# Six of the 31 taps of one depthwise convolution, moved from VectorE to float32 products with diagonal matrices on TensorE

## The chip, the core and the metric

The kernel runs on one core of a Trainium2 chip. The core has five engines that work side by side, each through its own queue in order: TensorE (PE; its weight loads are listed apart as PEld), VectorE (DVE), ScalarE (ACT), GpSimd (POOL) and SyncE (SP), which issues the DMAs. They share an on-chip memory (SBUF); TensorE writes its sums into a second one (PSUM), which VectorE and ScalarE read. The metric is device time in microseconds (us), the median of several runs.

## The reference

Two layers of a streaming encoder over 1024 prompt frames and 8 x 16 sample frames, model width 1024. Each layer computes, cut to what matters here:

```python
h = rms_norm(x, g1)
q, k, v, a, b = split(h @ w_in)
u = a * sigmoid(b)                              # 512 channels
A = sink_attention(q, k, v)                     # 8 heads, chunks of 64 frames, window 128
y = depthwise_conv31(u, conv_w) + conv_b        # causal, 31 taps, each channel by itself
C = silu(layer_norm(y))
x = x + concat(beta_a * A, beta_c * C) @ w_out
x = x + relu(rms_norm(x, g2) @ w_up) ** 2 @ w_down
```

The depthwise convolution is `y[c, t] = sum_k w[k, c] * u[c, t + k] + b[c]`, with 30 frames of state ahead of the first. For a fixed k it is the product of a 128x128 diagonal matrix, w[k] on the diagonal, with the 128 channels' frames shifted by k.

## The kernel before

Activations lie transposed, channels on the 128 partitions, frames along the free dimension. The 1152 frames are three blocks (b = 0, 1, 2) of 384. Everything is float32; for the large products each operand is split into a rounded part and a remainder (`h[0]`, `h[1]`; `u[:, 0]`, `u[:, 1]`), and `gemm` (L213 to L215) runs three one-pass products for each 128 rows of depth, 24 products of 128x384 for one output tile. A weight tile arrives by DMA (L204), ScalarE rounds it (L205), GpSimd takes the remainder (L206); six buffers hold the halves.

The first layer begins with `rmsnorm` of blocks 0 and 1 (L268 to L285). Then, by the program's text: `glu` of block 0 (eight gemms, the gate, the tile U of 4 channel tiles with 30 frames of halo ahead; L320 on GpSimd writes it), `make_qkv` of blocks 0 and 1, the attention of both, `glu` of blocks 1 and 2, `out(0)` (the product with w_out, then the norm `rmsnorm` of block 0 for the feed-forward), and the feed-forward of block 0 as filler.

The convolution is a generator that runs beside this in a "lane". `unit_done` is called after each gemm's unit of work and calls `tick`, which lets the generator at the head of each lane take `rate` steps: 6 for the first block of layer 0, 5 and 3 for the others (`CONV`). A step is one `yield`. In the kernel before, a step is one tap: a VectorE instruction that multiplies 384 shifted frames by the tap's weight (one scalar per partition) and adds them to the accumulator `acc` in PSUM. Tap 0 (L353) also adds the bias. After tap 30 ScalarE copies the accumulator over the first 384 columns of U (L358). The accumulator (tag "c") has one buffer, so the next channel tile waits for that copy. Four channel tiles of 31 taps make a block; then `conv_tail` does the layer norm and the SiLU, with the mean as a float32 product on TensorE (L659).

The text above isn't the order in which the engines work. The framework plans each engine's order ahead of the run from dependencies, the program's order as priority and its own estimates of durations (`schedule_with_timeline_sim=True`); the run then keeps that order on every engine. `after(t, self.pe)` orders a tap in this plan behind the latest gemm, without a wait in the run.

`hidden` (L704 to L707) is the first user of the tag "hid" (four buffers of 128x768), in the feed-forward.

Of the kernel before, what the change touches and what calls it, by code (L numbers as in the profile page):

```python
# [8 lines left out]
F32 = mybir.dt.float32  # L9
F32R = mybir.dt.float32r  # L10
AF = mybir.ActivationFunctionType
ALU = mybir.AluOpType
# [4 lines left out]
NCONV, CW, CS = 512, 31, 30  # L17
HD, NH, NKV = 64, 8, 2
EPS = 1e-6
NB, BT = 3, 384  # L20
# [15 lines left out]
MIX = ((0, 1, 1), (2, 0.9, 1.1))  # L36

CONV = ((6, 5, 3), (3.5, 3.5, 3.5))
TAIL = (3, 2)
ATT = ((0.5, 0.3, 0.3), (0.3, 0.35, 0.25))  # L40


G1, G2, QG, KG = 0, 8, 16, 17
CWT, CB, LNG, LNB = 18, 142, 146, 150
# [17 lines left out]
class Kernel:  # L62
# [235 lines left out]
    def glu(self, l, b, h, conv=None):  # L298
# [32 lines left out]
        if not last:  # L331
            self.halo = self.sp.tile([128, 4, CS], F32, tag="halo", name=self.nm("halo"), bufs=1)
            nc.gpsimd.tensor_copy(self.halo, U[:, :, BT:])

    def conv(self, l, b):

        nc = self.nc
        U = self.u[b]
        for ct in range(4):
            u = U[:, ct]  # L340
            if b < NB - 1:
                parts = [(lambda k: u[:, k:k + BT], slice(0, BT), lambda t: t)]
            else:
                us = u[:, UP:].rearrange("p (b s) -> p b s", s=SEG)
                parts = [(lambda k: u[:, k:k + 256], slice(0, 256), lambda t: t),
                         (lambda k: us[:, :, k:k + DEC_T], slice(256, BT), lambda t: t.rearrange("p (b s) -> p b s", s=DEC_T))]
            acc = self.pc()
            for k in range(CW):
                w = self.v(l, CWT + ct * CW + k)
                for src, s, view in parts:  # L350
                    o = view(acc[:, s])
                    if k == 0:
                        t = nc.vector.tensor_scalar(out=o, in0=src(k), scalar1=w, scalar2=self.v(l, CB + ct), op0=ALU.mult, op1=ALU.add)  # L353
                    else:
                        t = nc.vector.scalar_tensor_tensor(out=o, in0=src(k), scalar=w, in1=o, op0=ALU.mult, op1=ALU.add)  # L355
                    self.after(t, self.pe)
                if k == CW - 1:
                    nc.scalar.copy(u[:, :BT], acc)  # L358
                yield
        for _ in self.conv_tail(l, b):  # L360
            for _ in range(TAIL[l]):
                yield
# [659 lines left out]
    def run(self):  # L1022
        nc, tc, a = self.nc, self.tc, self.a
# [7 lines left out]
        x = [self.load_x(src[0])]  # L1031
        self.load_consts()
        x.append(self.load_x(src[1]))
        h1 = [self.rmsnorm(x[0], 0, G1), self.rmsnorm(x[1], 0, G1)]
        for l in range(DEPTH):
            self.u, self.co, self.k, self.vb = [None] * NB, [None] * NB, [], []
            x, h, ao = [None] * NB, [None] * NB, [None] * NB
            fin = l == DEPTH - 1
            nsrc = [a["y"][b] if fin else self.dp.tile([128, KT, BT], F32, tag=f"x{b}", name=f"xd{l}{b}") for b in range(NB)]
            kept = self.dp.tile([128, KT, BT], F32, tag=f"kept{l}", name=f"kept{l}")  # L1040
            nh = []
            alone, pair, place, mix, conv, att = (t[l] for t in (ALONE, PAIR, PLACE, MIX, CONV, ATT))

            def blk(b, end=False, x=x, h=h, nsrc=nsrc, nh=nh, l=l, fin=fin):
# [14 lines left out]
            with tc.tile_pool(name=f"ap{l}", bufs=1) as self.ap:  # L1059
                self.mix = 0  # L1060
                self.mix = mix[0]
                self.glu(l, 0, h1[0], conv)
                if l == 0:
                    for n in ("sk", "sv", "sc"):
# [3 lines left out]
                if l:  # L1068
                    self.glu(l, 1, h1[1], conv)
# [78 lines left out]
            h1, src = nh, nsrc  # L1148
# [120 lines left out]
```

## Time and profile before

| what | value |
|---|---|
| runs, median of 3 | 2387.7 us (2385.42 to 2388.78) |
| the profiled execution: its time, its span | 2387.42 us, 2385.6 us |
| PE busy | 2312.7 us, 97% of the span |
| DVE, POOL, ACT busy | 1676.6 us (70%), 1514.6 us (63%), 1269.3 us (53%) |
| mean granted TensorE clock | 0.995 of full speed |
| DMA | 266.49 MB, mean 112 GB/s |

The span is the time from the first to the last instruction in the trace; the execution's time is 1.8 us longer. A busy share is an average over the whole span; the work differs from stage to stage. Products overlap in TensorE, so that its busy time runs high: a gemm product lasts about 0.34 us by itself, while the next starts 0.17 us later. In a busy time by stretches, a column holds the busy us of one engine and, in brackets, its instructions. In a row of a timeline, the bracket at the end is the idle time of the engine just before and what ended it. "r", "g", "c" and "m" are tiles in PSUM, "f" and "t" scratch in SBUF.

### The profile page before, as it was taken

The page shows a single profiled execution, that of the slowest core. Times are in us where ns is not written, and L with a number is a line of the kernel's source. Part 1 is how long each engine was busy: PE and PEld are TensorE (multiplying, and loading weights), DVE is VectorE, ACT ScalarE, POOL GpSimd, SP SyncE. Part 2 cuts the span into 40 slices and gives each one's busy share as a digit, 9 for nine tenths or more (in the row PEclk, how much of TensorE's full clock was granted, in tenths as well). Part 3 has the DMA queues.
Part 4 walks back from the last instruction along what each step waited for, and adds up shares of the span by engine and source line. Part 5 has one row for each costly group of instructions (what it writes and reads, how often), then busy time and mean ns, then how long its engine had stood idle before and what let it go on. Part 6 is the DMA issues. An engine that isn't in the chain of part 4 may idle for free.

```text
span 2385.6 us, 39001 instructions
## 1 busy us (share of the span) xinstructions
PE 2312.7 (97%) x13822; PEld 2250.2 (94%) x13822; DVE 1676.6 (70%) x3153; ACT 1269.3 (53%) x2732; POOL 1514.6 (63%) x1247
## 2 busy tenths in 40 slices
PE   7999899999999999999999999999999999999999
PEld 7898898999989999999999999999999899999999
DVE  5999978996378777787687764799834877752222
ACT  5467546555335555644565566466433555544442
POOL 6975485656476665866856866856345666666662
PEclk9999999999999999999999999999999999999999
DMA  5423333434332223443334344434333122254442
GB/s 191 147 88 103 106 111 121 120 121 125 99 96 79 64 71 107 150 135 115 99 119 122 120 142 129 134 99 126 92 106 107 58 71 71 84 164 137 136 126 75
DMA packets 164260, 266.49 MB, mean 112 GB/s; under 512 B 24753, under 2 KB 55729, under 8 KB 164017
## 3 DMA queue, kind: packets, MB, share of 16 engines
q1 hardware_dynamic: 164064, 264.01, 35.8%
q8 instruction: 108, 1.77, 0.3%
q14 instruction: 88, 0.71, 0.1%
HBM read 250.19 MB, written 16.05 MB: 112 GB/s over the span
## 4 chain that ended last, share of the span: by engine, by line
PE 73%; DVE 18%; POOL 4%; issue 3%; DMA 2%; ACT 1%; DVEq 0%; POOLq 0%; SPq 0%; ACTq 0%
PE g L723 13%; PE g L213 12%; PE g L214 12%; PE g L215 12%; DVE c L355 6%; PE x L1006 4%; PE x L926 4%; PE g L1006 3%; PE m L723 2%; PE r L723 2%; PE g L926 2%; POOL w L893 2%; DMA A<-in_w 1%; PE c L723 1%; POOL w L206 1%
## 5 line engine op out<-in xcount | busy, mean ns | idle before, releaser
L206 POOL TENSOR_TENSOR w<-raw,w 128x512 fp32r<-128x512 f32 x728 | 972.7, 1347 | 599.5 <-ACT w L205 589.1
L205 ACT CAST w<-raw 128x512 fp32r<-128x512 f32 x728 | 445.1, 619 | 422.8 <-PE g L215 124.0
L213 PE MATMUL g<-h,w 128*128 128x384 f32 x1696 | 576.4, 341 | 8.2 <-ACT h L284 4.2
L214 PE MATMUL g<-h,w 128*128 128x384 f32 x1696 | 574.1, 339 | 0.6 <-DVE h L285 0.6
L215 PE MATMUL g<-h,w 128*128 128x384 f32 x1696 | 573.1, 338 | 0.0
L355 DVE SCALAR_TENSOR_TENSOR c<-u,vec,c 128x384 f32<-128x384 f32 (+1 forms) x960 | 498.0, 519 | 17.6
L723 PE MATMUL g<-hid,w 128*128 128x384 f32 x2304 | 429.1, 340 | 8.4 <-DVE x L725 5.3
L723 PEld LDWEIGHTS g<-hid,w 128*128 128x128 f32 x2304 | 397.8, 188 | 16.6 <-DVE x L725 9.5
L213 PEld LDWEIGHTS g<-h,w 128*128 128x128 f32 x1696 | 321.0, 189 | 12.4 <-ACT h L284 4.8
L214 PEld LDWEIGHTS g<-h,w 128*128 128x128 f32 x1696 | 321.0, 189 | 2.2 <-DVE h L285 1.0
L215 PEld LDWEIGHTS g<-h,w 128*128 128x128 f32 x1696 | 320.8, 189 | 0.9
L707 DVE TENSOR_TENSOR hid<-t,hid 128x384 fp32r<-128x384 f32 x128 | 107.5, 840 | 186.7 <-ACT hid L706 186.4
L893 POOL TENSOR_TENSOR w<-S,w 128x512 fp32r<-128x512 f32 x96 | 138.6, 1446 | 120.6 <-ACT w L892 120.3
L725 DVE TENSOR_TENSOR x<-x,g 128x384 f32<-128x384 f32 x240 | 130.0, 549 | 66.9 <-PE g L723 66.1
L704 ACT ACTIVATE t<-g 128x384 f32<-128x384 f32 x128 | 62.8, 491 | 148.2 <-PE g L215 147.7
L1006 PE MATMUL x<-F,w 128*128 128x384 f32 x624 | 120.4, 337 | 4.2 <-DVE x L1009 2.3
L893 POOL TENSOR_TENSOR w<-raw,w 128x512 fp32r<-128x512 f32 x64 | 90.5, 1414 | 41.9 <-ACT w L892 40.6
L1006 PEld LDWEIGHTS x<-F,w 128*128 128x128 f32 x624 | 109.3, 188 | 6.0 <-DVE x L947 2.5
L1006 PE MATMUL g<-F,w 128*128 128x384 f32 x528 | 107.6, 339 | 3.3 <-ACT F L815 1.4
L892 ACT CAST w<-S 128x512 fp32r<-128x512 f32 x96 | 59.7, 622 | 93.3 <-DVE S L879 48.2
L1006 PEld LDWEIGHTS g<-F,w 128*128 128x128 f32 x528 | 92.7, 188 | 7.1 <-ACT F L815 2.7
L893 POOL TENSOR_TENSOR w<-A,w 128x512 fp32r<-128x512 f32 x64 | 86.9, 1362 | 19.3 <-ACT w L892 19.1
(237 smaller groups left out, 4010.9 us busy)
## 6 DMA issues: line engine op xcount, KB each, us to landing
raw<-in_w SPq DMA_DIRECT2D x792, 256.0 KB, 2.7
A<-in_w SPq DMA_DIRECT2D x64, 256.0 KB, 2.7
x<-in_x SPq DMA_DIRECT2D x24, 384.0 KB, 5.0
x<-xd SPq DMA_DIRECT2D x12, 384.0 KB, 5.1
kept<-x SPq DMA_DIRECT2D x4, 768.0 KB, 4.0
x<-kept SPq DMA_DIRECT2D x8, 384.0 KB, 4.4
xd<-x SPq DMA_DIRECT2D x4, 768.0 KB, 4.9
out_y<-x SPq DMA_DIRECT2D x4, 768.0 KB, 4.4
```

The source lines that it names most:

```text
L205: nc.scalar.copy(u[:, 0], raw)
L206: nc.gpsimd.tensor_tensor(out=u[:, 1], in0=raw, in1=u[:, 0].bitcast(F32), op=ALU.subtract)
L213: nc.tensor.matmul(ps, lhsT=u(0, k), rhs=h(0, k), start=k == 0, stop=False)
L214: nc.tensor.matmul(ps, lhsT=u(0, k), rhs=h(1, k), start=False, stop=False)
L215: self.pe = nc.tensor.matmul(ps, lhsT=u(1, k), rhs=h(0, k), start=False, stop=k == KT - 1)
L355: t = nc.vector.scalar_tensor_tensor(out=o, in0=src(k), scalar=w, in1=o, op0=ALU.mult, op1=ALU.add)
L707: nc.vector.tensor_tensor(out=hid[:, 1], in0=f, in1=hid[:, 0].bitcast(F32), op=ALU.subtract)
L723: self.pe = nc.tensor.matmul(ps, lhsT=u(p), rhs=hid[:, q], start=i == 0, stop=i == n - 1)
L725: nc.vector.tensor_tensor(out=x[:, m], in0=x[:, m], in1=ps, op=ALU.add)
L893: nc.gpsimd.tensor_tensor(out=u[:, 1], in0=f[n], in1=u[:, 0].bitcast(F32), op=ALU.subtract)
L926: nc.tensor.matmul(ps, lhsT=u[:, p, k], rhs=H[h](q, k), start=start and k == 0 and i == 0, stop=k == 3 and i == 2, skip_group_check=True)
L1006: nc.tensor.matmul(o, lhsT=u[:, p, 2 * i + j], rhs=F(j, hn)[:, q], start=start and n == 0, stop=n == 5, skip_group_check=True)
```

## The change

Before the norm of block 1, `diagonal` builds four tiles of six 128x128 diagonal matrices, one for each channel tile: the identity times the weights of taps 0 to 5, both spread by broadcasting, in one VectorE instruction of 128x768. They lie in the four "hid" buffers. The convolution of layer 0, block 0, which is the first to find `self.diagonals` filled, takes for each channel tile one entry: six float32 products add taps 0 to 5 into the accumulator, VectorE adds taps 6 to 30 as before, and the copy becomes an activation that adds the bias. There is one more `yield` behind the products of each tile, and one ahead of the first tile. All other convolutions find the list empty and stay as they are.

```diff
--- before.py
+++ after.py
@@ -36,6 +36,7 @@
 MIX = ((0, 1, 1), (2, 0.9, 1.1))
 
 CONV = ((6, 5, 3), (3.5, 3.5, 3.5))
+TAPS = 6
 TAIL = (3, 2)
 ATT = ((0.5, 0.3, 0.3), (0.3, 0.35, 0.25))
 
@@ -332,6 +333,14 @@
             self.halo = self.sp.tile([128, 4, CS], F32, tag="halo", name=self.nm("halo"), bufs=1)
             nc.gpsimd.tensor_copy(self.halo, U[:, :, BT:])
 
+    def diagonal(self, ct):
+
+        n = TAPS * 128
+        d = self.hp.tile([128, 2, BT], F32R, tag="hid", name=self.nm("dg"), bufs=4).bitcast(F32).rearrange("p a b -> p (a b)")[:, :n].rearrange("p (k c) -> p k c", c=128)
+        w = self.v(0, CWT + ct * CW, TAPS)
+        self.nc.vector.tensor_tensor(out=d, in0=self.ident.unsqueeze(1).to_broadcast([128, TAPS, 128]), in1=w.unsqueeze(2).to_broadcast([128, TAPS, 128]), op=ALU.mult)
+        return d
+
     def conv(self, l, b):
 
         nc = self.nc
@@ -345,7 +354,15 @@
                 parts = [(lambda k: u[:, k:k + 256], slice(0, 256), lambda t: t),
                          (lambda k: us[:, :, k:k + DEC_T], slice(256, BT), lambda t: t.rearrange("p (b s) -> p b s", s=DEC_T))]
             acc = self.pc()
-            for k in range(CW):
+            taps = TAPS if self.diagonals else 0
+            if taps:
+                if ct == 0:
+                    yield
+                dg = self.diagonals.pop(0)
+                for k in range(taps):
+                    nc.tensor.matmul(acc, lhsT=dg[:, k], rhs=u[:, k:k + BT], start=k == 0, stop=k == taps - 1)
+                yield
+            for k in range(taps, CW):
                 w = self.v(l, CWT + ct * CW + k)
                 for src, s, view in parts:
                     o = view(acc[:, s])
@@ -355,7 +372,10 @@
                         t = nc.vector.scalar_tensor_tensor(out=o, in0=src(k), scalar=w, in1=o, op0=ALU.mult, op1=ALU.add)
                     self.after(t, self.pe)
                 if k == CW - 1:
-                    nc.scalar.copy(u[:, :BT], acc)
+                    if taps:
+                        nc.scalar.activation(u[:, :BT], acc, AF.Identity, bias=self.v(l, CB + ct))
+                    else:
+                        nc.scalar.copy(u[:, :BT], acc)
                 yield
         for _ in self.conv_tail(l, b):
             for _ in range(TAIL[l]):
@@ -1031,7 +1051,9 @@
         x = [self.load_x(src[0])]
         self.load_consts()
         x.append(self.load_x(src[1]))
-        h1 = [self.rmsnorm(x[0], 0, G1), self.rmsnorm(x[1], 0, G1)]
+        h1 = [self.rmsnorm(x[0], 0, G1)]
+        self.diagonals = [self.diagonal(ct) for ct in range(4)]
+        h1.append(self.rmsnorm(x[1], 0, G1))
         for l in range(DEPTH):
             self.u, self.co, self.k, self.vb = [None] * NB, [None] * NB, [], []
             x, h, ao = [None] * NB, [None] * NB, [None] * NB
```

## Rows read from the trace of the kernel before

**Rows 1.** The page: engine, busy us (share), instructions; the chain; a line's group.

```profile
PE 2312.7 (97%) x13822; PEld 2250.2 (94%) x13822; DVE 1676.6 (70%) x3153; ACT 1269.3 (53%) x2732; POOL 1514.6 (63%) x1247
...
PE 73%; DVE 18%; POOL 4%; issue 3%; DMA 2%; ACT 1%; DVEq 0%; POOLq 0%; SPq 0%; ACTq 0%
...
L206 POOL TENSOR_TENSOR w<-raw,w 128x512 fp32r<-128x512 f32 x728 | 972.7, 1347 | 599.5 <-ACT w L205 589.1
```

**Rows 2.** Busy us (instructions) of PE, PEld, DVE, ACT, POOL by stretch; granted clock, DMA.

```profile
25.00:75.00 50.00, 50.00 (x298) 49.69 (x297) 35.38 (x65) 28.74 (x51) 40.14 (x30) 1.00 0.58 187
75.00:186.00 111.00, 106.66 (x750) 98.59 (x748) 107.75 (x215) 67.71 (x177) 94.78 (x90) 0.97 0.32 97
186.00:290.00 104.00, 92.02 (x565) 87.22 (x565) 99.85 (x206) 67.79 (x167) 50.65 (x46) 0.94 0.37 111
300.00:540.00 240.00, 232.49 (x1450) 223.11 (x1450) 214.16 (x493) 140.02 (x351) 154.78 (x142) 1.00 0.39 118
```

**Rows 3.** The chain that ended last, by line, 25 to 75 us.

```profile
by line: PE g L214 32.5%; PE g L215 31.8%; PE g L213 31.6%; PE r L249 2.2%; PE r L255 1.2%; PE g L382 1.1%; PE g L445 0.4%
```

**Rows 4.** The chain that ended last, by line, 75 to 186 us.

```profile
by line: DVE c L355 43.3%; DVE t L295 6.4%; issue 6.3%; DVE t L293 6.1%; DVE h L285 4.8%; DVE t L292 4.0%; DVE f L283 4.0%; DVE s L500 3.9%; DVE s L503 3.0%; DVE s L506 2.6%; DVE pt L560 2.6%; DVE s L502 2.0%; DVE v L429 1.7%; DVE ao L574 1
```

**Rows 5.** The line of taps 1 to 30, 50 to 192 us: count, ns min/median/max.

```profile
L355 DVE SCALAR_TENSOR_TENSOR c<-u,vec,c x120: 594/622/624, 52.5 to 189.9; 128x384 f32<-128x384 f32 x120
```

**Rows 6.** The line of tap 0, 50 to 192 us.

```profile
L353 DVE TENSOR_SCALAR c<-u,vec x4: 668/670/680, 50.9 to 164.4; 128x384 f32<-128x384 f32 x4
```

**Rows 7.** ScalarE's copies of the accumulator, 50 to 200 us.

```profile
L358 ACT COPY u<-c x4: 468/476/491, 85.9 to 191.5; 128x384 f32<-128x384 f32 x4
```

**Rows 8.** VectorE in order of time: start us, us, instruction, idle before.

```profile
71.00 3.26 DVE L355 SCALAR_TENSOR_TENSOR c<-u,vec,c 128x384 f32<-128x384 f32 x5
75.36 0.62 DVE L283 SCALAR_TENSOR_TENSOR f<-x,vec,r 128x384 f32<-128x384 f32 x1 [1.10 <-PE r L255]
```

**Rows 9.** TensorE in order of time around the float32 product L659.

```profile
204.33 0.34 PE L214 MATMUL g<-h,w 128*128 128x384 f32 x1
204.51 0.81 PE L659 MATMUL r<-f,cst 128*128 128x384 f32 x2
204.86 0.63 PE L215 MATMUL g<-h,w 128*128 128x384 f32 x1
205.33 0.33 PE L213 MATMUL g<-h,w 128*128 128x384 f32 x1
```

**Rows 10.** Who TensorE waited for, 50 to 290 us: total us, times, longest.

```profile
PE m L568 <- DVE pt L560: 4.3, 4, 2.7
...
PE g L213 <- DVE s L446: 2.7, 1, 2.7
...
PE m L558 <- DVE og L572: 2.0, 5, 0.5
```

**Rows 11.** VectorE in order of time at the start.

```profile
8.82 0.17 DVE L179 TENSOR_SCALAR nsk<-vec 128x12 f32<-128x12 f32 x1
9.81 0.96 DVE L272 TENSOR_TENSOR f<-f,f 128x768 f32<-128x768 f32 x1 [0.82 <-ACT f L268]
10.81 0.56 DVE L273 TENSOR_TENSOR f<-f 128x384 f32<-128x384 f32 x1
12.90 0.16 DVE L220 TENSOR_SCALAR s<-r 128x3 f32<-128x3 f32 x1 [1.53 <-PE r L249]
```

**Rows 12.** VectorE in order of time, the second block's norm.

```profile
33.26 1.65 DVE L273 TENSOR_TENSOR f<-f 128x384 f32<-128x384 f32 x1
```

**Rows 13.** TensorE in order of time around its longest wait.

```profile
94.64 0.69 PE L213 MATMUL g<-h,w 128*128 128x384 f32 x1 [2.65 <-DVE s L446]
95.13 0.52 PE L214 MATMUL g<-h,w 128*128 128x384 f32 x1
95.45 0.52 PE L215 MATMUL g<-h,w 128*128 128x384 f32 x1
```

**Rows 14.** Busy time by stretches, the ten us around that wait.

```profile
90.00:100.00 10.00, 7.22 (x43) 6.75 (x43) 9.90 (x23) 4.01 (x9) 9.77 (x11) 0.66 0.28 80
```

## The prediction

> **What bounds the kernel now.** I read the page first, then the stretch in which the change sits. On the page TensorE is busy 97% of the span and the chain of work that ended last runs 73% on it, 18% on VectorE [rows 1]. An average like that hides stages, so the next view is the busy time by stretches [rows 2]. From 25 to 75 us TensorE has no idle time at all. From 75 to 186 us TensorE idles 111 - 106.7 = 4.3 us and VectorE 3.3 us: both are full. From 186 to 290 us TensorE idles 12.0 us, VectorE 4.2 us. The granted clock there is 0.97 and 0.94, which takes 0.03 x 111 = 3.3 us and 0.06 x 104 = 6.2 us more of full-speed work away. So TensorE's slack between 75 and 290 us is 4.3 + 12.0 + 3.3 + 6.2 = 25.8 us, and between 300 and 540 us, with VectorE less loaded, it is 7.5 us of 240, or 3.1%.
>
> The chain by lines says which of two full engines sets the pace. From 25 to 75 us it lies on the gemm (L213 to L215, 96%) [rows 3]. From 75 to 186 us it lies on VectorE from end to end, and the convolution's taps are its largest part, 43.3% [rows 4]; TensorE's gemms don't appear. So the stretch is VectorE's from 75 to 186 us and TensorE's before it; behind it, up to 290 us, both idle some, and I take it as shared.
>
> The first block's convolution is 4 first taps (L353, 0.67 us) and 120 more (L355, 0.62 us) between 50.9 and 190 us [rows 5, 6]; its four results are copied by ScalarE between 85.9 and 191.5 us, 0.48 us each [rows 7].
>
> **Part 1: taps taken from VectorE.** Of 124 taps 100 stay, all of the L355 kind, so 4 at 0.67 and 20 at 0.62 us go: 15.1 us. What they are worth depends on place. The six of the first channel tile ran from 51 us on, while the chain lay on TensorE [rows 3], and at 75.36 us VectorE waits 1.1 us for a TensorE result [rows 8], so what it saved by then is lost in a longer wait. I count them at nothing. The 18 of the other three tiles lie on the chain: 3 x 0.67 + 15 x 0.62 = 11.3 us gained.
>
> **Part 2: products put on TensorE.** 24 float32 products of 128x384. The trace has one kind like it: the mean of the convolution's tail (L659) is float32 by float32, 128x384. It stands as two records; from its start at 204.51 us to the start of the second gemm product behind it at 205.33 us there are 0.82 us, of which one gemm product takes 0.17 (the spacing of its neighbours), so 0.65 us a product [rows 9]. 24 x 0.65 = 15.6 us, against 15.1 us freed: the change moves work, it doesn't save any. The first tile's six, 3.9 us, land between 50 and 60 us, where TensorE has no idle time [rows 2]: +3.9 us. The other 18, 11.7 us, are covered by the slack of 25.8 us. If that cover were gone, they would cost the whole 11.7 us.
>
> Check from TensorE's side: its work from 75 to 290 us is 215 - 25.8 = 189.2 us; with 11.7 more it is 200.9. At the idle share of 300 to 540 us, 3.1%, that takes 207.3 us, a gain of 7.7 us, less the 3.9 us ahead of it: -3.8 us. With no idle time at all it would be -14.1 + 3.9 = -10.2 us, which is the most that the change can give before 290 us; with today's idle time kept, +15.6 us.
>
> **Part 3: waits that are new.** VectorE's seventh tap now waits for six products, and these wait for the copy of the tile before, since the accumulator has one buffer. The copy is there today. New in each of three changes of tile are six products, 3.9 us, and whatever stands ahead of them in TensorE's queue. Queued behind the waiting tap are the attention's softmax, rope and norm instructions of VectorE; the planner may place these ahead of it. Bounds: nothing, if 3.9 us of such work is ready each time (the rest of the chain's 56.7% in [rows 4] says that it is plentiful), and 3 x 3.9 = 11.7 us if none is. Nearer to the first: 1 us each, 3 us. TensorE's waits for VectorE and ScalarE today are mostly short (five of L558 give 2.0 us) [rows 10], so I take that the new ones are too.
>
> **Part 4: building the matrices.** Four VectorE products of 128x768. The nearest rows are additions of the same size at 0.96 us [rows 11]: 3.8 us. They depend only on the constants, which the instruction at 8.82 us already uses, and VectorE has gaps of 0.8 to 1.5 us in the start's chain of norm steps, between 7 and 16 us. Each gap takes about one; with 0.96 us in a gap of 0.8 to 1.0 us they overhang a little. I take 0.7 us of delay (at least 0, at most 3.8, all of them in a row on the path). A later place is dearer: the addition of two halves, 128x384, took 0.56 us at 10.81 us and 1.65 us at 33.26 us [rows 11, 12], when GpSimd was splitting weights. The Trainium skill (SBUF — State Buffer, section "SBUF: two separate sides") says why: a VectorE instruction with two SBUF inputs and GpSimd share one port pair under an exclusive lock. The two rows bear it out. By that page four matrices built beside the splitting would each wait up to one splitting, 1.35 us [rows 1], 5.4 us in all, and the sum would end at +1 us.
>
> **Part 5: the rest.** The copy becomes an activation with a bias. The trace has no such form; were it twice the copy's 0.48 us [rows 7], that is 0.48 us more four times, on ScalarE, which is busy 67.7 of the 111 us [rows 2]: nothing (1.9 us uncovered). The matrices sit in the four "hid" buffers, whose first user, `hidden`, needs the norm of block 0 and so this very convolution: nothing. No DMA is added. A channel tile now takes 26 steps of the lane and the first 27, instead of 31, so the tail is emitted some three ticks earlier; that changes the order, at nothing in the mean.
>
> **Sum.** -11.3 + 3.9 + 3 + 0.7 = -3.7 us by VectorE's side, -3.8 + 0.7 = -3.1 by TensorE's. From 300 us on the work is the same, so I pass it on whole. Against the profiled execution's 2387.4 us (its span is 2385.6) that is 2383.7 us; the median of the runs is 2387.7, 0.3 us above, so I say 2384.
>
> **Rivals.** (a) *Head of the queue, slower.* Place: the three changes of tile. A product set in TensorE's order where the plan thinks VectorE done, but where VectorE is late, holds up the gemms behind it. The trace has such a case: until 94.64 us TensorE waited 2.65 us on VectorE (L446), and then ran gemm products 0.32 us apart instead of 0.17, the lower level of 1.2 GHz; the mean granted clock from 90 to 100 us is 0.66 [rows 13, 14]. Price: the wait, 2.65 us, and at most 10 x 0.34 = 3.4 us of lost clock, 6 us together. One such case gives 2390, two 2396, three 2402. I put the rival at 2395. It decides from 3.7 / 3 = 1.2 us a change of tile on, beyond the 1 us already counted. Against it: short waits in [rows 10]. The Trainium skill (TensorE: Matmul & The Clock Gate, section "Part 3: Packing small matmuls") states the rule under it, that matmuls start and end in program order and only weight loads go ahead; the wait in [rows 13] agrees.
>
> (b) *TensorE takes over, no change.* The gain on VectorE is given back because TensorE, now the fuller engine, keeps waiting here and there for VectorE, ScalarE and the weights. Its idle share is 3.9% from 75 to 186 us and 11.5% from 186 to 290 us today [rows 2]; at 5% after the change the stretch takes 200.9 / 0.95 = 211.5 us, 3.5 less than today, and with 3.9 and 0.7 ahead of it the sum is +1: 2388.5 us. For it: three engines are near full at once, GpSimd is busy 94.8 of the 111 us. Against it: 3.1% where VectorE is less loaded.
>
> (c) *Relief is passed on, more gain.* VectorE stays 89% busy to 540 us [rows 2], so taps done earlier move the second block's convolution forward and the steps from 200 to 290 us, where TensorE waits 4.3 us for L560 in four waits [rows 10] and idles 12 us, close up. Then TensorE's idle time before 290 us goes to nothing, -10.2 us by the check above, and with 0.7 for the matrices the time is about 2378.
>
> **Numbers.** A measurement of this kernel tells 0.2%, 4.8 us, from no change. Chances: forecast (gain of 2 to 7 us, 2381 to 2386) 0.40, of which 0.17 is beyond 4.8 us; (a) 0.24, of which 0.22 slower; (b) 0.18, of which 0.04 slower; (c) 0.18, faster. Faster 0.35, within 0.39, slower 0.26. The range goes from (c) to (a) and leaves out the far end of each: 2375 to 2396.
>
> **What would show it.** In the changed profile: 24 new products of about 0.65 us in pairs of records; taps of the first block x100 at 0.62 us; the last of its copies by about 184 us instead of 191.5; the chain between 75 and 186 us with more TensorE in it; TensorE's idle time from 75 to 290 us down to some 7 us. Rival (a) shows as TensorE idle ahead of these products, ended by the accumulator's copy, with a granted clock below 1.00 behind it. The prediction is wrong if the products last well over 0.65 us, if VectorE idles ahead of the seventh tap by more than 1 us each, or if the planner orders later stages in another way.

## The result and the profile after

| | before | after |
|---|---|---|
| median of 3 runs, us | 2387.7 | 2405.7 (2405.35 to 2407.03) |
| ratio, 95% interval | 1 | 1.0081 [1.0063, 1.0099] |
| span of the profiled execution, us | 2385.6 | 2405.2 |
| first gemm product starts, us | 17.9 | 21.9 |
| first hidden unit of the feed forward cast, us | 300.9 | 324.4 |

The kernel became 18 us slower, past the upper end of the predicted range (2396). All of the loss is there when the feed-forward begins: its first hidden unit is 23.5 us late, and the end 19.6 us by the spans.

The page after, which answers to [rows 1]: busy us and share of each engine, then the chain that ended last.

```profile
PE 2328.4 (97%) x13870; PEld 2261.1 (94%) x13870; DVE 1673.7 (70%) x3133; ACT 1271.1 (53%) x2732; POOL 1511.4 (63%) x1247
...
PE 77%; DVE 13%; POOL 3%; DMA 2%; issue 2%; ACT 2%; SPq 0%; DVEq 0%; POOLq 0%; ACTq 0%
```

TensorE's busy time grew by 15.7 us and VectorE's fell by 2.9. Of the chain 4 points more lie on TensorE and 5 fewer on VectorE. The stretches of [rows 2], in the kernel after (its stages run later, so a stretch doesn't hold quite the same work as before):

```profile
25.00:75.00 50.00, 50.00 (x283) 48.31 (x283) 36.21 (x61) 28.75 (x48) 36.22 (x28) 1.00 0.50 170
75.00:186.00 111.00, 106.27 (x700) 94.63 (x699) 96.00 (x190) 62.37 (x158) 82.87 (x79) 0.98 0.26 89
186.00:290.00 104.00, 95.90 (x606) 91.27 (x605) 88.82 (x169) 67.52 (x172) 52.98 (x51) 0.92 0.35 108
```

From 75 to 186 us TensorE is as full as it was (106.3 of 111 us), but with fewer instructions, 700 against 750; VectorE went from 107.8 to 96.0 us. The chain by line in the same stretch, which answers to [rows 4]:

```profile
by line: PE g L214 14.8%; PE g L216 14.4%; PE g L215 13.9%; PE c L363 10.8%; DMA raw<-in_w 7.9%; DVE c L372 7.9%; DVE t L296 4.2%; issue 3.7%; PE g L465 3.5%; DVE t L294 3.2%; PE s L553 2.7%; DVE t L293 2.6%; PE m L588 1.8%; PE r L410 1.7%;
```

The stretch changed hands. Before, 43% of it were taps on VectorE; now 43% are gemm products (L214 to L216) and 11% the new products (L363), with 8% taps (L372). The new products, by their line, with who waited for them (DVE is VectorE):

```profile
L363 PE MATMUL c<-u,dg x48: 483/485/590, 53.3 to 170.1; 128*128 128x384 f32 x48
...
  DVE c L372: 3.8, 2
```

They stand as 48 records, two for each product, and a set of six takes 3.58 to 4.07 us from its first start to the next other product's start. VectorE waited for them twice, 3.8 us in all. The start on VectorE, which answers to [rows 11], and the same microseconds on GpSimd:

```profile
8.68 3.56 DVE L341 TENSOR_TENSOR dg<-cst,vec 128x768 f32<-128x768 f32 x4
12.16 0.95 DVE L273 TENSOR_TENSOR f<-f,f 128x768 f32<-128x768 f32 x1
...
18.11 0.17 DVE L241 TENSOR_TENSOR r<-s,r 128x3 f32<-128x3 f32 x1 [2.64 <-POOL s L232]
```

```profile
13.53 3.74 POOL L207 TENSOR_TENSOR w<-raw,w 128x512 fp32r<-128x512 f32 x3 [10.65 <-DMA raw<-in_w]
17.23 0.85 POOL L232 TENSOR_TENSOR s<-s,half 128x3 f32<-128x3 f32 x1
```

The four matrices don't spread over the gaps: they run in one block, and the addition of the first norm that stood at 9.81 us slips to 12.16. By then GpSimd has weights to split and does three splits before the norm's power (L232), for which VectorE waits 2.64 us, where it waited 0.96 before. So the first gemm product is 4.0 us late: 2.35 us from the block and 1.68 from this wait.

### The profile page after: what moved, and what is told of

Its sections match the earlier page's. It is cut to its first block, busy times and chain, and to the rows that moved or that the text cites. A ratio compares the mean times of both kernels' runs of the same rounds, so it can differ in the third digit from the quotient of the medians.

```text
span 2405.2 us, 39083 instructions
## 1 busy us (share of the span) xinstructions
PE 2328.4 (97%) x13870; PEld 2261.1 (94%) x13870; DVE 1673.7 (70%) x3133; ACT 1271.1 (53%) x2732; POOL 1511.4 (63%) x1247
## 4 chain that ended last, share of the span: by engine, by line
PE 77%; DVE 13%; POOL 3%; DMA 2%; issue 2%; ACT 2%; SPq 0%; DVEq 0%; POOLq 0%; ACTq 0%
PE g L743 13%; PE g L214 13%; PE g L216 12%; PE g L215 12%; PE x L1026 4%; PE x L946 4%; DVE c L372 4%; PE g L1026 3%; PE g L946 3%; PE m L743 2%; PE r L743 2%; PE c L743 1%; PE s L553 1%; PE m L588 1%; POOL w L207 1%
## 5 line engine op out<-in xcount | busy, mean ns | idle before, releaser
L214 PE MATMUL g<-h,w 128*128 128x384 f32 x1696 | 576.6, 341 | 11.9 <-ACT t L318 4.6
L216 PE MATMUL g<-h,w 128*128 128x384 f32 x1696 | 573.0, 338 | 0.0
L372 DVE SCALAR_TENSOR_TENSOR c<-u,vec,c 128x384 f32<-128x384 f32 (+2 forms) x940 | 485.6, 517 | 21.7 <-PE c L363 3.8
L743 PEld LDWEIGHTS g<-hid,w 128*128 128x128 f32 x2304 | 399.4, 189 | 17.4 <-DVE x L745 11.7
L214 PEld LDWEIGHTS g<-h,w 128*128 128x128 f32 x1696 | 321.0, 189 | 16.7 <-ACT t L318 5.0
L216 PEld LDWEIGHTS g<-h,w 128*128 128x128 f32 x1696 | 320.6, 189 | 0.6
L913 POOL TENSOR_TENSOR w<-A,w 128x512 fp32r<-128x512 f32 x64 | 86.9, 1363 | 16.5 <-ACT w L912 16.3
```

What stands on the lines that cost most here:

```text
L214: nc.tensor.matmul(ps, lhsT=u(0, k), rhs=h(0, k), start=k == 0, stop=False)
L216: self.pe = nc.tensor.matmul(ps, lhsT=u(1, k), rhs=h(0, k), start=False, stop=k == KT - 1)
L743: self.pe = nc.tensor.matmul(ps, lhsT=u(p), rhs=hid[:, q], start=i == 0, stop=i == n - 1)
L913: nc.gpsimd.tensor_tensor(out=u[:, 1], in0=f[n], in1=u[:, 0].bitcast(F32), op=ALU.subtract)
```

## The experiments

Theory P: the stretch is TensorE's as much as VectorE's, so the products count at their price and the taps taken away bring nothing (e11, e12 and e14 to e17 call it W; W in e4, e10 and e13 is another theory). Rival V: the relief of VectorE is real, as predicted, and something else (the matrices, the waits at changes of tile) eats it. Rival O: neither work matters much; the planner, which sets the order of all instructions from its own estimates, makes another and worse order for the whole kernel. Sixteen kernels tell them apart; each expectation says what its letters stand for. Each ratio below is against the kernel before, run on the same chip.

**Parts of the change, each in an order that the planner makes anew.**

```diff
-            for k in range(CW):
+            first = 6 if l == 0 and b == 0 else 0
+            for k in range(first, CW):
```

> The kernel before, with taps 0 to 5 of the first block of layer 0 left out (25 taps remain, the bias goes into the first of them), no products and no matrices: VectorE's relief by itself. Theory P (TensorE sets the pace of the whole stretch to 300 us, its idle time is latency of waits, VectorE's relief is worth next to nothing): 2384 to 2388 us, and the first conv copy of the last channel tile earlier by 10 us or more all the same. Rival V (VectorE sets the pace from 75 to 186 us as the chain says, so its relief is worth its 11 to 15 us, and something new ate it in the changed kernel): 2373 to 2377 us.

Measured 2418.0, 1.0125 [1.0108, 1.0142]. Taking work away, and adding none, cost 30 us. That fits neither P nor V. The stretch of [rows 2] in this kernel, and one row of GpSimd in it:

```profile
75.00:186.00 111.00, 85.33 (x531) 75.00 (x530) 98.92 (x210) 61.88 (x160) 57.76 (x56) 0.77 0.19 58
```

```profile
168.37 0.74 POOL L423 MEMSET v<- 128x768 f32 x1 [37.20 <-PE m L569]
```

In the new order GpSimd stands 37.2 us at the clearing of the attention's v, whose buffer TensorE still uses. The weight splits are queued behind it, so TensorE has no gemm to run, is busy 85.3 of 111 us and at a granted clock of 0.77. It is the order that shows here, not the work; e13 below settles it.

The second run puts the 31 taps back and keeps products and matrices:

```diff
-            for k in range(taps, CW):
+            for k in range(CW):
```

> The changed kernel with all 31 taps still on VectorE: tap 0 overwrites what the products have summed, and the bias goes in with it, so that products and matrices are pure addition. Theory P: as the changed kernel, 2404 to 2409 us, since the taps put back cost nothing. Rival V: the changed kernel and the 11 to 15 us of the taps, 2416 to 2421 us.

Measured 2405.8, 1.0073 [1.0058, 1.0088], which is the changed kernel's time within the intervals, and not V's 2416 to 2421. As far as two kernels with orders of their own can be compared, the 24 taps that the change takes away are worth nothing in it.

The third builds the matrices at the head and uses none (`taps = 0`):

> The changed kernel with its matrices built and never used: 31 taps on VectorE, no products. Both theories: the start is late by what the four instructions do to the first norm; the first gemm product stands at 21.9 us in place of 17.9, so 2390 to 2392 us if that is passed on whole; 2388 if TensorE catches it up while it waits for weights.

Measured 2397.1, 1.0037 [1.0024, 1.0050]. That is 8.8 us by the ratio, above both expectations, which had the 4 us of the start at most.

The fourth is the change with shorter products:

```diff
-                    nc.tensor.matmul(acc, lhsT=dg[:, k], rhs=u[:, k:k + BT], start=k == 0, stop=k == taps - 1)
+                    n = BT if k == 0 else 128
+                    nc.tensor.matmul(acc[:, :n], lhsT=dg[:, k], rhs=u[:, k:k + n], start=k == 0, stop=k == taps - 1)
```

> The changed kernel with the products of taps 1 to 5 cut to 128 of 384 columns (the rest of these taps' sums is left out): same instructions, waits and matrices, but about 20 x 0.42 = 8.4 us less of TensorE's time. Theory P: 2405.7 - 8 = 2396 to 2399 us. A theory W, that the waits and the order of the new products cost it and not their length: 2403 to 2406 us.

Measured 2401.8, 1.0059 [1.0044, 1.0074]: it lies between what P and W expected, and decides nothing by itself.

The fifth gives a channel tile 31 steps of its lane again, as before the change, with empty steps behind the products:

> The changed kernel with empty lane steps behind the products, so that a channel tile takes 31 steps as before and the tail of the first convolution is emitted at the same tick as before. Theory P (the products' time on TensorE is the cost): as the changed kernel, 2403 to 2408 us. Theory O (the cost lies in the order that the planner makes of fewer steps, a tail that comes early and is put ahead of gemms): 2390 to 2398 us, and the second half of block 2's gates no longer 35 to 41 us late.

Measured 2411.4, 1.0101 [1.0085, 1.0116], above both expectations. The steps given back don't bring the time back. The sixth orders the matrices behind the first block's norm (`self.after(t, self.normed)`):

> The changed kernel with the four matrices ordered behind the last instruction of block 0's norm on VectorE. The first gemm product should stand at 17.9 us again, not at 21.9. Theory P: 2.4 to 4 us less than the changed kernel, 2401 to 2403 us. Theory O: anything within 10 us of it, since the order changes again.

Measured 2408.2, 1.0084 [1.0069, 1.0099], though the first gemm product is back at 17.9 us: above P's 2403, and no more than O allowed. The seventh is the kernel before with taps 1 to 6 cut to 64 columns, and the next, as a test of the planner, the kernel before with one empty step (`yield`) ahead of the first tap:

> The kernel before with taps 1 to 6 of the first block of layer 0 cut to 64 of 384 columns (the other columns of these taps are left out): same number of instructions and lane steps, but about 24 x 0.4 = 10 us less of VectorE's time. It is the clean form of the run with taps left out. Theory P (TensorE's waits are latency): 2385 to 2389 us. Rival V (VectorE's relief is worth what the chain shows): 2377 to 2380 us. Theory O: not told apart if the order of the gemms moves.

> The kernel before with one empty lane step ahead of the first convolution, and nothing else: no work is added or removed. Theory P and rival V: 2386 to 2390 us, no change. Theory O (the time follows the planner's order, whatever the work): 3 us or more to either side.

Measured 2401.5, 1.0054 [1.0039, 1.0069] for e7, and 2388.8, 1.0006 [0.9996, 1.0015] for e9. Again less work on VectorE is slower. The second says nothing on order: in its trace every engine's instructions stand in the order of the kernel before, so the step moved nothing.

**The same, with the order held.** These runs can't separate work from order. So the next eight take the order of the built program before, engine by engine, and chain the instructions of each engine to it by order-only dependencies:

```python
# line: one engine's instructions in the order of the kernel before
for x, y in zip(line, line[1:]):
    tc.add_manual_dep(y, x.name, DependencyInfo(NoSync, DATA), reason="held")
```

Added instructions are put at chosen places of these lists, removed ones drop out. The traces of e10 and e13 show that it works: all 13822 records of TensorE, and those of ScalarE, GpSimd and VectorE, stand in the order of the kernel before, the missing taps apart; in e7, with the work of e10, 755 places of TensorE's order hold another instruction.

```diff
+                if l == 0 and b == 0 and 1 <= k <= 6:
+                    yield
+                    continue
```

> The kernel before without taps 1 to 6 of each channel tile of block 0 (the convolution has 25 taps), as in e1_taps_only, with every engine's instructions held in the order of the kernel before. Theory O (order): 15 us less of VectorE work, at most 11.3 of them on the path, and no new order: 2376 to 2388 us, where e1 had 2418. Theory W (work): over 2400 us again.

> The kernel before with taps 1 to 6 of each channel tile of block 0 cut from 384 to 64 columns (the other 320 columns keep what was there), as in e7_short_taps, but with every engine's instructions held in the order of the kernel before. Theory O (order): what makes the runs slower is the order that the planner makes anew, so the 10 us less of VectorE work can't cost anything by itself: 2376 to 2388 us, and e7's 13 us are gone. Theory W (work): taking VectorE work away unsettles the engines whatever the order: about 2400 us again, as in e7.

Measured 2388.9, 1.0004 [0.9995, 1.0014] for e13 and 2388.7, 1.0005 [0.9997, 1.0014] for e10. Both lie just above O's range and 11 us below W's 2400. Two things follow. The 30 and 13 us that e1 and e7 lost were the planner's order, as theory O said. And 24 taps less on VectorE, in the order in which they were 43% of the chain, gain nothing (at most 1.2 us by the interval): rival V falls. Where the relief went is seen on VectorE by line, from 50 to 192 us: busy us, mean ns of one, idle before. First the kernel before, then e13, whose line of taps stands 4 later (its lane's steps stay, taps 1 to 6 are gone):

```profile
L355 DVE SCALAR_TENSOR_TENSOR c<-u,vec,c 128x384 f32<-128x384 f32 x120 | 74.0, 617 | 1.5
...
L295 DVE TENSOR_TENSOR t<-t,t 128x384 f32<-128x384 f32 x10 | 7.7, 777 | 0.1
...
L272 DVE TENSOR_TENSOR f<-f,f 128x768 f32<-128x768 f32 x3 | 2.9, 952 | 0.0
```

```profile
L359 DVE SCALAR_TENSOR_TENSOR c<-u,vec,c 128x384 f32<-128x384 f32 x96 | 59.3, 617 | 1.3
L295 DVE TENSOR_TENSOR t<-t,t 128x384 f32<-128x384 f32 x10 | 10.1, 1014 | 0.6 <-POOL t L294 0.5
...
L272 DVE TENSOR_TENSOR f<-f,f 128x768 f32<-128x768 f32 x3 | 3.9, 1301 | 2.3 <-ACT f L268 2.3
```

The waits of VectorE in e13 in the same stretch, total us, times, longest:

```profile
DVE s L504 <- PE s L537: 2.5, 1, 2.5
DVE f L272 <- ACT f L268: 2.3, 2, 1.3
DVE c L357 <- ACT u L362: 1.3, 1, 1.3
DVE f L283 <- PE r L255: 1.2, 1, 1.2
```

The taps shrank by 14.7 us (74.0 to 59.3). VectorE's eleven waits, of which the longest stand above, come to 10.2 us, where before there were two, 2.4 us; and its additions of two operands became longer, L295 by 2.4 us and L272 by 1.0. The convolution's fourth copy starts at 190.5 us instead of 191.5, the first hidden unit at 299.1 instead of 300.9. VectorE got to the next result sooner, and found TensorE, ScalarE or GpSimd not there yet. (The rest of the 14.7 us lies in smaller changes, not listed here.) The chain by line of e13, 75 to 186 us, says who:

```profile
by line: PE g L213 19.6%; PE g L215 19.2%; PE g L214 19.2%; issue 7.5%; PE s L537 5.9%; POOL w L206 5.0%; DVE t L295 4.0%; PE m L572 3.1%; PE g L449 2.8%; DMA raw<-in_w 2.7%; DVE t L293 1.9%; PE m L562 1.8%; PE r L430 1.2%; ACT w L205 1.1%;
```

The gemms, absent in [rows 4], are 58% of it. So a second chain, TensorE's, was all but as long as the one on VectorE.

The change itself with the order held: products where the copy of the tile before them ended, matrices in a gap of VectorE (4.0 us, from 41.4 us on), 24 taps gone:

> The change as a whole (24 products, 24 taps fewer, four matrices, the bias in the copy), with every other instruction held in the order of the kernel before on every engine; the matrices stand behind the norm of block 1, in a gap of VectorE, and the products of a channel tile stand in TensorE's order where the copy of the tile before them ended in the kernel before. Theory O (order): the change's 18 us come from the new order: 2380 to 2391 us. Theory W (work): the products' 15.6 us lie on TensorE's path whatever the order: 2399 to 2406 us.

And the same with all 31 taps kept:

> As e11_change_held, but with all 31 taps kept on VectorE (the first of them overwrites the products), so work is only added: 15.5 us on TensorE and 3.6 us of matrices on VectorE, with the order of the kernel before. Theory O (order): only the six products at 50 us, where TensorE has no idle time, and new waits at the changes of tile count: 2391 to 2397 us. Theory W (work): all of the 15.5 us count: 2402 to 2408 us.

Measured 2398.8, 1.0051 [1.0037, 1.0064] for e11, and 2401.4, 1.0058 [1.0045, 1.0072] for e12. Both lie within 0.7 us of W's range, and 4 us or more above O's. So products and matrices cost 12 to 14 us with the old order too, and the taps that they replace are worth 1.7 us (the difference of the two ratios), which is within their intervals. How much of the products TensorE's idle time took in is seen over the same work, from 75 us to the first hidden unit, which is cast at 300.9, 299.1, 312.8 and 329.8 us. In order: the kernel before, e13, e11, and e16, a run below with twice the products:

```profile
75.00:300.90 225.90, 209.58 (x1378) 196.67 (x1377) 217.29 (x434) 141.71 (x355) 150.28 (x140) 0.95 0.33 101
```

```profile
75.00:299.10 224.10, 207.46 (x1368) 195.80 (x1367) 212.23 (x416) 141.82 (x356) 149.33 (x139) 0.96 0.33 102
```

```profile
75.00:312.80 237.80, 224.98 (x1431) 207.87 (x1430) 211.14 (x420) 143.19 (x356) 149.64 (x140) 0.95 0.32 97
```

```profile
75.00:329.80 254.80, 241.37 (x1490) 219.95 (x1489) 216.25 (x436) 146.09 (x361) 153.50 (x144) 0.95 0.30 91
```

TensorE's idle time (the stretch less its first column) falls from 16.3 us to 12.8 in e11 and is 13.4 in e16. So some 3 us of idle time were filled, once, and the rest stayed. It consists of waits for other engines: in the kernel before the five largest of them, by line, come to 13.9 us of the 16.3, and the same five are still there in e11, with 10.2 us.

Four runs more size the parts. Matrices alone, held in the same gap:

> The kernel before with the four matrices built in VectorE's gap at 41 us and used by nothing, every other instruction held in the order of the kernel before. Theory W (TensorE's work sets the time): no work on TensorE, so nothing: 2386 to 2389 us. Theory M (the matrices are part of what e11 lost): 2390 us and more.

Measured 2391.0, 1.0012 [1.0003, 1.0021], so 2.9 us, as M said. They don't fit the gap:

```profile
41.60 6.15 DVE L339 TENSOR_TENSOR dg<-cst,vec 128x768 f32<-128x768 f32 x4
47.68 0.60 DVE L283 SCALAR_TENSOR_TENSOR f<-x,vec,r 128x384 f32<-128x384 f32 x1
```

The norm's step L283 starts at 47.68 us, where it started at 45.38 before.

Shorter and doubled products, both as e11 otherwise:

```diff
# e15
+                    n = 128 if k else BT
+                    t = nc.tensor.matmul(acc[:, :n], lhsT=dg[:, k], rhs=u[:, k:k + n], start=k == 0, stop=k == taps - 1)
# e16
-                for k in range(taps):
+                for k in [*range(taps), *range(taps)]:
```

> As e11_change_held, but taps 1 to 5 of each set are multiplied for 128 of 384 columns only (the other columns lack them), so the products of a tile take 0.65 + 5 x about 0.22 = 1.75 us instead of 3.9; the waits at the changes of tile stay. Theory W (the length of the products is the loss): 11.5 x 1.75 / 3.9 = 5 us over the kernel before, 2391 to 2394 us. Theory Q (the loss lies in the places of the queue where products and taps wait for each other): as e11, 2396 to 2400 us.

> As e11_change_held, but each set of six products is multiplied twice (the second time adds the same taps again), so TensorE gets 31 us instead of 15.5. Theory W: nearly all of the second 15.5 us count, 2411 to 2415 us. Theory S (slack of TensorE that the first set used in part still covers): 2399 to 2405 us.

(In e16 the second set starts the sum anew, so it replaces the first instead of adding to it; the work on TensorE is as told.) Measured 2394.2, 1.0024 [1.0015, 1.0033] for e15 and 2416.1, 1.0117 [1.0103, 1.0131] for e16. The four sets, each from its first start to the next other product's start, take 7.0 us in e15, 14.8 in e11 and 30.3 in e16. By the ratios (times 2388 us) the kernels lose 5.7, 12.2 and 27.9 us, each with 2 to 3 us of uncertainty. If the matrices are 2.9 us of it, as they are alone (e14), the first 7.0 us of products cost 2.8; the next 7.8 cost 6.5, and the next 15.5 cost 15.7. Past the 3 us of idle time that could be filled, the loss is the length of the products at its full price, and theory P stands. (e16 lies above W's range by 1 us.) The number of places where taps and products wait for each other is the same in all three.

The last puts e11's matrices where the changed kernel has them:

> As e11_change_held, but with the four matrices where the changed kernel has them, on VectorE ahead of the third square addition of the first norm, at about 9 us. Theory W: the first gemm product is 3 to 4 us later, and of that 2 to 4 us are left at the end: 2400 to 2403 us; what is left to the 2405.7 us of the changed kernel is the planner's order. Theory H (the whole difference between e11 and the changed kernel is the head): 2404 to 2407 us.

Measured 2404.0, 1.0071 [1.0059, 1.0084]: 17.0 us by the ratio, 4.8 more than e11. The two intervals together leave 4 us of doubt in this 4.8. Its first gemm product starts at 20.5 us, 2.6 us late and not 4.0: with the old order GpSimd does the norm's power ahead of its splits. W expected up to 2403, H from 2404, so the two can't be told apart; the interval overlaps that of the changed kernel, 1.0081 [1.0063, 1.0099].

| kernel | taps | products | matrices | order held: ratio | planner's order: ratio |
|---|---|---|---|---|---|
| before | 31 | none | none | 1 | 1 |
| taps gone (e13, e1) | 25 | none | none | 1.0004 | 1.0125 |
| taps short (e10, e7) | 31 | none | none | 1.0005 | 1.0054 |
| matrices alone (e14 at 41 us; e3 at the head) | 31 | none | four | 1.0012 | 1.0037 |
| matrices late (e11 at 41 us, e6 at 26 us) | 25 | 24 | four | 1.0051 | 1.0084 |
| matrices at the head (e17, the changed kernel) | 25 | 24 | four | 1.0071 | 1.0081 |

## Why the prediction was wrong

It failed in two steps, both on who sets the pace from 75 to 186 us.

*"The 18 of the other three tiles lie on the chain: ... 11.3 us gained."* They did lie on the chain, and gained nothing (e13: 1.0004). The chain tells which work ended last, not by how much. The bound stood in the same view: with TensorE busy 106.7 of 111 us [rows 2], no relief of VectorE can shorten this stretch by more than TensorE's 4.3 us of idle time and the 3.3 us that the prediction put down to the clock, unless TensorE's own work shrinks. I read both and then used them only as slack for new work. And a relieved VectorE didn't end TensorE's idle time: from 75 us to the first hidden unit it is 16.6 us in e13, as against 16.3.

*"The other 18, 11.7 us, are covered by the slack of 25.8 us."* A small part was: TensorE's idle time fell by 3.5 us in e11, and by 2.9 with twice the products (e16), whose second half cost all of its length. The slack was mostly waits for another engine's result, and the products, put where they were, left these waits standing. The 9.5 us of the 25.8 that were worked out from the clock didn't come back either: it is 0.95 over the same work in the kernel before, in e11 and in e16. The bound "with today's idle time kept, +15.6 us" was written down; less the 3.5 us it is 12.1, and e11 lost 12.2. Of 3.1% of idle time, taken from another stretch, nothing is seen.

Point by point. *Part 1, first tile:* its taps at nothing, as said. The last copy of the block, forecast by 184 us, starts at 194.5 us in the changed kernel and at 190.5 in e13. *Part 2, price of a product:* 0.65 us [rows 9] was right: six products more make a set 7.45 - 3.58 = 3.87 us longer (e16), 0.645 us each. *Part 3, waits of 3 us:* VectorE waited 3.8 us in two waits. That they cost nothing is likely, as relief of VectorE is worth nothing (e13), but no run shows it alone. *Part 4, matrices at 0.7 us:* mis-sized. In the changed kernel they cost 4.0 us at the first gemm product, since they ran as one block ahead of the norm's addition, and GpSimd's splits came in ahead of the norm's power. At the end they cost 4.8 us more at the head than in the gap at 41 us (e17 less e11), where they cost 2.9 by themselves (e14): 7.7 us together, and 8.8 alone in the planner's order (e3). The bound of 3.8 us was too low; it left out the second queue, and why the end loses more than the first gemm product isn't settled. The gap at 41 us is no free place either: there the four took 6.15 us instead of 3.80, 2.35 more, where the prediction's estimate for such a place was up to 5.4. *Part 5:* the copy with a bias took 0.58 us in place of 0.48, and with 31 steps kept (e5) the change is no faster. Later stages in another order, named as a sign of being wrong, cost 30 and 13 us in e1 and e7, but in the change itself little that can be told (2.3 us, e17).

So of 19.3 us by the ratio, 12.2 are the products with the matrices in a gap (of which 2.9 are what the matrices cost there alone, e14), 4.8 the matrices' place at the head, and 2.3 the planner's order, within the uncertainty of both ratios. Rival (b), TensorE as the bound, names the mechanism, but with a size of 1 us, since it still granted VectorE's gain. Rival (a) is not seen: TensorE waited 0.2 us ahead of all the products together, and its longest wait was no product's, but a gemm's for an activation of the gate (L318), 4.6 us until 219.8 us.

```profile
PE g L214 <- ACT t L318: 4.6, 1, 4.6
```

Not settled is whether some order other than that of before could make use of the relief, or whether products placed inside TensorE's waits would cost less; every held run puts them where a copy ended. In the four pairs of the table with the same work (e13 and e1, e10 and e7, e11 and e6, whose matrices stand apart, e17 and the changed kernel) the planner's own order was never better than the held one. No version beat the kernel before.

## What to carry to other kernels

In this kernel two engines were both over 95% busy in a stretch, and the chain of waits named one of them. It tells which work ended last, not by how much: look up the other engine's idle time there before counting on relief. Work given to the other engine filled some 3 of 16 us of idle time and then counted at full price; show which wait it fills before calling it covered. Where a planner orders the instructions from its own estimates, an edit can be two edits, of work and of order: hold the old order to price the work (here e1 and e13, the same work 29 us apart), before reading a reason out of the new time. And see in the trace whether the order moved at all (in e9 it didn't). Work that was ready early and looked free was put at the head as one block here, and what it delayed lost its turn in a second engine's queue as well.

## What the runs showed of the hardware

Here VectorE's instructions with two inputs in SBUF have no fixed length. In e13 the same ten additions L295 took 1014 ns instead of 777 in the mean. The matrices show it best: 951 ns each at the head, where GpSimd stood idle until 13.53 us, and this at 41 us (e14) beside its weight splits (ns min/median/max):

```profile
L339 DVE TENSOR_TENSOR dg<-cst,vec x4: 945/1697/2045, 41.6 to 45.7; 128x768 f32<-128x768 f32 x4
```

GpSimd's three splits beside them took 1.66 us and twice 2.0 us, where the one before took 1.29. The taps, which read the accumulator in PSUM and a scalar beside one input in SBUF, kept 617 ns in the mean in e13 and in the kernel before. The Trainium skill (SBUF — State Buffer, section "SBUF: two separate sides") says that VectorE and GpSimd share a port pair under an exclusive lock; these rows agree. By them VectorE's busy time holds some waiting that the busy share doesn't show; how much of the stretch from 75 to 186 us that is, no run shows.

A float32 product of 128x384 holds TensorE for 0.645 us, in two records, against 0.17 us for a gemm product of the same shape [rows 9]. A set of one long product and five of 128 columns took 1.68 us instead of 3.58.
